# First MLP products of an encoder trunk by seven half-size products in place of eight

## The chip, the cores and the metric

The kernel runs on one core of a Trainium2 chip. A core has TensorE (PE, matrix products; PEld in the profile is its loading of stationary operands), VectorE (DVE), ScalarE (ACT), GpSimd (POOL) and SyncE (SP), and 16 DMA engines which take transfers issued by SP, ACT and POOL. The metric is the time of one execution on the device in microseconds (us), the median of several runs.

## The reference

A two-layer trunk on 512 tokens of width 1024, all in float32. Layer 0 mixes by a conformer convolution, layer 1 by latent attention under a chunk mask. After its mixer each layer has the same kind of MLP, with 4096 hidden columns; the change concerns its first product.

```python
def squared_relu_mlp(h, w1, w2):
    return jnp.square(jax.nn.relu(h @ w1)) @ w2

for layer in range(DEPTH):
    ...
    m = conformer_conv(hn, ...) if layer < N_A_LAYERS else mla_attention(hn, ...)
    h = h + rms_norm(m, mix_post_g[layer])
    f = squared_relu_mlp(rms_norm(h, ffn_pre_g[layer]), w_ff1[layer], w_ff2[layer])
    h = h + rms_norm(f, ffn_post_g[layer])
```

## The kernel before

**Operands in two parts.** TensorE multiplies numbers in a reduced float format (`F32R`). Each operand is therefore kept as a high part and a low part (`split`, line 791: ScalarE writes the high part, VectorE source minus high), and a product is three matmuls: high x high, low x high, high x low. A weight block of 128 x 1024 floats (512 KB) is loaded from `wts` into a tile `raw`, and split into `wh` and `wl` (`weight`, line 733). For the blocks named by `lo_by_dma` (line 88), ScalarE writes both the high part and its negative, and a DMA on POOL's queue adds the block from memory onto the negative, which gives the low part without VectorE.

**Order.** `Program` records every instruction and plans the order before it is issued. TensorE keeps the order in which the program was recorded; each other engine is ordered by due times that are worked back from TensorE's (`due`, line 408, and `schedule`, line 451), with written-out costs for each operation. An operation recorded with two engines (`nc.binary`) goes to the one that would end it first by these costs. All instructions are issued in one helper, line 640, and so the profile shows that line for all of them; groups are told apart by the names of their tiles.

**Buffers.** Tiles belong to tags with a fixed number of places. `raw` (5 places), `wh` (5) and `wl` (6) are taken in turn: a block may be loaded or split only when the block as many places earlier is done with. `USE` lists the weights in the order in which the products take them. `big` (48 tiles of 128 x 512) holds activations, their parts, the convolution's Toeplitz blocks (loaded from `cw`) and the accumulators; `row` (2 of 128 x 1024) holds gains and a bias repeated along the tokens. `mm` is six banks of PSUM.

**The MLP** (`feed_forward`, line 963). The hidden columns go in four groups q of 1024. For each q come first the first products: eight blocks m of 128 columns, for each 8 steps over the 1024 input columns x 3 matmuls, with 512 tokens in each (operand names `mm<-big,wh` and `mm<-big,wl`, moving operand first). In q = 0 the blocks m = 0 to 3 are done in two halves of 256 tokens, because the later half of the normed input X is not there yet; these four blocks get their low parts by DMA. ScalarE applies relu and square into `Z`, eight tiles by token half, column half and u.

Then come that group's second products (names `mm<-wh,big`): Z times the second weight matrix, two by two quarters in seven products of Strassen's kind (`STRASSEN`, `PRODUCTS`). Their left sides are differences of Z tiles made and split by VectorE and ScalarE (`terms`), their right sides are sums of two weight blocks: a plus by a second, accumulating DMA on POOL's queue, a minus by a second `raw` tile and VectorE. In q = 0 ScalarE copies a product into an accumulator in `big`, later VectorE adds onto it (`collect`). A group has 24 loads of 512 KB for its second products, 8 of them accumulating, and 8 for its first.

`post_norm` (line 1065) takes the results, multiplies them by a row of gains (`row`, line 873) and adds them to the residual `h`. `prenorm` transposes and norms `h` into X half by half of the tokens; its last VectorE operation for a half is `SCALAR_TENSOR_TENSOR big<-bc,vt,big`.

Of the kernel before, what the change touches and what calls it, by code (L numbers as in the profile page):

```python
# [8 lines left out]
F32 = mybir.dt.float32  # L9
F32R = mybir.dt.float32r  # L10
# [12 lines left out]
DH = 512  # L23
RMS_EPS = 1e-6
# [98 lines left out]

def _ff(layer):
    for q in range(4):
        for m in range(8):
            _blk(("ff1", layer, q, m))
# [516 lines left out]
def trunk(ctx: ExitStack, tc: tile.TileContext, xT, xN, wts, vec, along, rope, cw, out):  # L644
# [13 lines left out]
    RAW = tag("raw", 5, [P, D], fifo=True)  # L658
    ROW = tag("row", 2, [P, D])
    for t in (RAW, ROW):  # L660
        for place in range(1, t.count):
            t.make(f"{t.name}_", F32, place)
# [7 lines left out]
    BIG = tag("big", 48, [P, T])  # L670
# [61 lines left out]

    def weight(key):

        while key not in blocks:
            name, parts = USE[len(blocks)]
            i, n = BLK[parts[0][0]], _cols[BLK[parts[0][0]]]
# [109 lines left out]
    def sums(parts, t0, dim):  # L847
# [11 lines left out]
    def rsqrt_bc(accs, t0, n, dim, eps, dst=None):  # L859

        nb = n // P
        sm = sums([(b, acc, b) for acc in accs for b in range(nb)], t0, dim)
# [7 lines left out]

    HALVES = {HA: (0, 1), HB: (2, 3)}
# [35 lines left out]
    def residual(F, g, b, dh, o, st, on, r2):  # L907
# [5 lines left out]
        nc.binary(on, out=F[b][dh], in0=F[b][dh], in1=g[:, dh * DH : (dh + 1) * DH], op=ALU.mult)  # L913
# [48 lines left out]

    def feed_forward(layer, X, F):
# [5 lines left out]
        both = {}  # L969
        for q in range(4):  # L970

            Z = {(th, kh): [big() for _ in range(2)] for kh in range(2) for th in range(2)}
            order = [(m, FULL) for m in range(8)]
            if q == 0:
                order = [(m, t) for t in (HA, HB) for m in range(4)] + order[4:]
            for m, (t0, n) in order:
                pt = products(("ff1", layer, q, m), X, t0, n)
                s = slice(t0, t0 + n)
                z = tmp()
                nc.scalar.activation(z[:, s], pt[:, :n], AF.Relu)  # L980
                for th, (a, w) in enumerate((HA, HB)):
                    if t0 <= a < t0 + n:
                        j = m % 2
                        nc.scalar.activation(
# [713 lines left out]
```

## Time and profile before

| | us |
|---|---|
| median of 3 runs | 1059.95 |
| lowest and highest | 1058.62, 1062.92 |
| profiled execution | 1060.22 |
| its span, first to last instruction | 1058.4 |
| layer 0: first products of q = 0 start | 195.26 |
| second products of q = 0 start | 241.97 |
| first products of q = 1 start | 280.05 |
| second products of q = 1 start | 323.57 |
| first products of q = 2 start | 361.65 |

The mean granted TensorE clock is 0.997 of full speed. The starts are read from the timeline of TensorE, where the names of the operands change places. A matmul's line shows start, length and count: matmuls overlap, so that the distance between starts, not the length, is what one costs. A window's line shows, for a stretch, the time in which each engine was busy. A group's line shows how many instructions of one kind there were, their busy time together and the mean length of one in ns, and then the idle time ahead of them with what ended it.

### The profile page before, as it was taken

How to read it: one execution, taken by the hardware profiler on the slowest of the kernel's cores; microseconds unless marked ns; L12 is line 12 of the kernel's file. 1: busy time of each engine (PE TensorE's matmuls, PEld its weight loads, DVE VectorE, ACT ScalarE, POOL GpSimd, SP SyncE). 2: the span in 40 equal slices, each digit the busy share in tenths (PEclk: the TensorE clock that was granted, in tenths of full speed). 3: DMA queues.
4: the chain of work that ended last, by engine and by line, in shares of the span. 5: the costliest groups of instructions: out<-in, count | busy, mean ns of one | idle time of the engine just before them, and what ended most of it. 6: DMA issues, size and time to landing. Idle time of an engine off the chain costs nothing.

```text
span 1058.4 us, 15181 instructions
## 1 busy us (share of the span) xinstructions
PE 1037.9 (98%) x5284; PEld 883.2 (83%) x5284; DVE 763.0 (72%) x1559; ACT 641.6 (61%) x1343; POOL 141.5 (13%) x165
## 2 busy tenths in 40 slices
PE   8999999999999999999999999999999999999996
PEld 7888988988888888888788888889888888888885
DVE  6498994857448738959988977447574495498698
ACT  8552596867556445555767877558575554455652
POOL 1110001101100100002105533301010010000010
PEclk9999999999999999999999999999999999999998
DMA  8996898658857948658822132567598488586694
GB/s 281 319 250 192 271 254 217 163 142 235 250 150 213 259 131 253 180 176 235 225 64 89 56 102 81 177 181 177 162 250 248 119 237 256 148 242 172 180 244 133
DMA packets 67613, 204.08 MB, mean 193 GB/s; under 512 B 7632, under 2 KB 13904, under 8 KB 67536
## 3 DMA queue, kind: packets, MB, share of 16 engines
q1 hardware_dynamic: 49680, 150.15, 41.3%
q0 software_dynamic: 13536, 49.29, 25.7%
q10 hardware_dynamic: 4320, 3.68, 1.1%
q8 instruction: 41, 0.67, 0.3%
q14 instruction: 36, 0.29, 0.1%
HBM read 197.58 MB, written 5.51 MB: 192 GB/s over the span
## 4 chain that ended last, share of the span: by engine, by line
PE 85%; DVE 7%; DMA 3%; ACT 3%; issue 1%; DVEq 0%; ACTq 0%
PE mm L640 82%; DVE big L640 5%; PE bc L640 3%; DMA raw<-wts 2%; ACT big L640 2%; DVE stat L640 1%; DVE wl L640 1%; ACT wh L640 1%; ACT wl L640 1%; DMA uu<-dealt 1%; DMA dealt<-big 1%; DVE tmp L640 0%; ACT tmp L640 0%; DVE h L640 0%; DMA vt<-vec 0%
## 5 line engine op out<-in xcount | busy, mean ns | idle before, releaser
L640 PE MATMUL mm<-big,wh 128*128 128x512 f32 (+1 forms) x1512 | 440.6, 374 | 1.1 <-ACT wh L640 1.1
L640 PE MATMUL mm<-wh,big 128*128 128x512 f32 (+1 forms) x1216 | 372.2, 385 | 0.0
L640 ACT ACTIVATE wh<-raw 128x512 fp32r<-128x512 f32 (+2 forms) x444 | 251.4, 614 | 121.6 <-PE mm L640 73.5
L640 PEld LDWEIGHTS mm<-big,wh 128*128 128x128 f32 x1512 | 276.8, 189 | 50.8 <-ACT wh L640 1.4
L640 DVE TENSOR_TENSOR wl<-raw,wh 128x512 fp32r<-128x512 f32 (+1 forms) x356 | 227.2, 679 | 105.9 <-ACT wh L640 105.5
L640 PE MATMUL mm<-big,wl 128*128 128x512 f32 (+1 forms) x756 | 282.4, 374 | 0.0
L640 PEld LDWEIGHTS mm<-wh,big 128*128 128x128 f32 x1216 | 226.1, 188 | 44.2 <-ACT wh L640 0.2
L640 PE MATMUL mm<-wl,big 128*128 128x512 f32 (+1 forms) x608 | 233.4, 385 | 0.0
L640 PEld LDWEIGHTS mm<-big,wl 128*128 128x128 f32 x756 | 143.1, 189 | 24.6 <-DVE wl L640 0.5
L640 PEld LDWEIGHTS mm<-wl,big 128*128 128x128 f32 x608 | 114.2, 188 | 22.5 <-DVE wl L640 0.4
L640 POOL DMA_DIRECT2D raw<-wts x64 | 55.5, 867 | 568.1 <-DVE wl L640 194.3
L640 ACT ACTIVATE big<-tmp 128x256 f32<-128x256 f32 (+1 forms) x208 | 95.8, 493 | 47.5 <-DVE tmp L640 41.5
L640 DVE TENSOR_TENSOR big<-big,big 128x512 f32<-128x512 f32 (+4 forms) x103 | 69.7, 697 | 55.2 <-ACT big L640 54.9
L640 ACT ACTIVATE tmp<-mm 128x512 f32<-128x512 f32 (+1 forms) x75 | 41.7, 555 | 101.4 <-PE mm L640 100.2
L640 PE MATMUL mm<-big,big 128*128 128x256 f32 (+3 forms) x520 | 83.5, 310 | 1.9 <-DVE big L640 1.9
L640 PEld LDWEIGHTS mm<-big,big 128*128 128x128 f32 x520 | 73.1, 190 | 7.0 <-DVE big L640 2.4
L640 ACT ACTIVATE big<-mm 128x512 f32<-128x512 f32 (+5 forms) x106 | 56.6, 537 | 32.0 <-PE mm L640 30.8
L640 DVE TENSOR_TENSOR big<-tmp,big 128x512 fp32r<-128x512 f32 (+1 forms) x96 | 60.7, 640 | 15.3 <-ACT big L640 12.7
L640 DVE SCALAR_TENSOR_TENSOR big<-big,vt,big 128x512 fp32r<-128x512 f32 (+29 forms) x95 | 63.2, 728 | 5.7 <-ACT big L640 5.7
L640 DVE TENSOR_TENSOR big<-big,mm 128x512 f32<-128x512 f32 x96 | 63.2, 679 | 2.4 <-PE mm L640 2.3
L640 DVE TENSOR_TENSOR tmp<-big,big 128x512 f32<-128x512 f32 x80 | 53.2, 684 | 8.8 <-ACT big L640 8.7
L640 POOL DMA_DIRECT2D wl<-wts x30 | 26.1, 869 | 210.0 <-ACT wl L640 168.7
(90 smaller groups left out, 769.3 us busy)
## 6 DMA issues: line engine op xcount, KB each, us to landing
raw<-wts SPq DMA_DIRECT2D x222, 512.0 KB, 4.9
raw<-wts POOLq DMA_DIRECT2D x64, 512.0 KB, 8.1
wl<-wts POOLq DMA_DIRECT2D x30, 512.0 KB, 8.5
big<-cw SPq DMA_DIRECT2D x45, 256.0 KB, 5.5
big<-wts SPq DMA_DIRECT2D x12, 256.0 KB, 4.3
row<-along SPq DMA_DIRECT2D x5, 512.0 KB, 5.5
raw<-wts SPq DMA_DIRECT2D x12, 192.0 KB, 2.8
big<-xT SPq DMA_DIRECT2D x8, 256.0 KB, 4.6
```

Source lines behind the costliest of these rows:

```text
L640: return f(*args, **kwargs)
```

## The change

In each layer the first products of q = 0 and q = 1 are now computed ahead of all second products of that layer. The eight blocks of a group are regrouped into two units u of 512 hidden columns, with weight blocks of 512 input columns by 256 hidden columns (`w1`, four to a unit, the same bytes as before). The first unit of a layer (q = 0, u = 0) is computed plainly in halves of 256 tokens. The other three units are computed by Winograd's form of Strassen's product: seven products of 512 input columns x 256 hidden columns x 256 tokens. Three of these (1, 2, 4) take a single weight block, and they come first; four (5, 7, 6, 3) take sums that VectorE forms in place in the `raw` tiles. Products 1 and 2 get their low parts by DMA. The combinations of X are formed once per layer, after the plain unit has been recorded: 16 sums of high and low part on POOL or VectorE, 8 operations on VectorE and 16 splits of 256 columns. VectorE and ScalarE combine the seven products, with relu and square, into the same Z tiles.

To hold this, `raw` grows from 5 to 8 places, `big` shrinks from 48 to 46, and the tag `row` goes: a row is now two tiles of `big`, loaded when the first result is taken up. q = 2 and q = 3 stay as they were. The rest of the diff renames a helper, moves a definition and lays out the weights.

```diff
+H = 256
...
-    if name[0] == "ff1":
-        return name[2] == 0 and name[3] < 4
+    if name[0] == "w1":
+        return name[2:4] == (0, 0) or name[4] in LO_BY_DMA
...
+QUADS = ((0, 0), (0, 1), (1, 0), (1, 1))
+EARLY = (0, 1)
+PLAIN = {1: (0, 0), 2: (0, 1), 4: (1, 1)}
+WINOGRAD = (1, 2, 4, 5, 7, 6, 3)
+LO_BY_DMA = (1, 2)
+def _first(layer, q):
+    n = len(USE)
+    for u in range(2):
+        for mh, kh in QUADS:
+            _blk(("w1", layer, q, u, mh, kh))
+    del USE[n:]
+    for u in range(2):
+        for key in QUADS if (q, u) == (0, 0) else WINOGRAD:
+            USE.append((("w1", layer, q, u, key), None))
 def _ff(layer):
+    for q in EARLY:
+        _first(layer, q)
     for q in range(4):
-        for m in range(8):
+        for m in range(8 if q not in EARLY else 0):
...
-    RAW = tag("raw", 5, [P, D], fifo=True)
-    ROW = tag("row", 2, [P, D])
+    RAW = tag("raw", 8, [P, D], fifo=True)
...
-    BIG = tag("big", 48, [P, T])
+    BIG = tag("big", 46, [P, T])
...
+    sums = {}
+    def first_weight(name):
+        _, layer, q, u, key = name
+        def at(mh, kh):
+            return wts[BLK["w1", layer, q, u, mh, kh]]
+        def load(part):
+            t = nc.tile(RAW)
+            nc.sync.dma_start(out=t, in_=at(*part))
+            return t
+        if isinstance(key, tuple):
+            raw, src = load(key), at(*key)
+        elif key in PLAIN:
+            raw, src = load(PLAIN[key]), at(*PLAIN[key])
+            sums[key] = raw
+        else:
+            if key == 5:
+                sums[5], sums[7] = sums[4], load((1, 0))
+            if key == 6:
+                sums[6] = sums[5]
+            if key == 3:
+                sums[3] = sums[6]
+            raw = sums[key]
+            nc.vector.tensor_tensor(out=raw, in0=raw, in1=sums[{5: 7, 7: 1, 6: 1, 3: 2}[key]], op=ALU.add)
+        hi, lo = nc.tile(WH, F32R), nc.tile(WL, F32R)
+        if lo_by_dma(name):
+            for dst, scale in ((lo, -1.0), (hi, 1.0)):
+                nc.scalar.activation(dst, raw, AF.Copy, scale=scale)
+            nc.gpsimd.dma_start(out=lo, in_=src, accum_op=ALU.add)
+        else:
+            split(raw, slice(0, D), (hi, lo))
+        return hi, lo
...
     def row(name):
-        t = nc.tile(ROW)
+        ts = [big() for _ in range(2)]
         nc.early = 30000.0
-        nc.sync.dma_start(out=t, in_=along[ROWS.index(name)])
+        for dh, t in enumerate(ts):
+            nc.sync.dma_start(out=t, in_=along[ROWS.index(name), :, dh * DH : (dh + 1) * DH])
         nc.early = 0.0
-        return t
+        return ts
...
+    def combinations(X):
+        raw = {}
+        for kh, th in QUADS:
+            for kp in range(2):
+                a = raw[kh, th, kp] = big()
+                for j in range(2):
+                    hi, lo = (x[:, th * H : (th + 1) * H].bitcast(F32) for x in X[4 * kh + 2 * kp + j])
+                    nc.binary(("gpsimd", "vector"), out=a[:, j * H : (j + 1) * H], in0=hi, in1=lo, op=ALU.add)
+        out = {p: [] for p in WINOGRAD}
+        for k, (hi, lo) in enumerate(X):
+            out[1 if k < 4 else 2].append((hi[:, :H], lo[:, :H]))
+            if k > 3:
+                out[3].append((hi[:, H:], lo[:, H:]))
+        def put(p, c):
+            for j in range(2):
+                x = big(F32R)
+                out[p].append((x[:, :H], x[:, H:]))
+                split(c, slice(j * H, (j + 1) * H), out[p][-1], slice(0, H))
+        c7 = [tmp() for _ in range(2)]
+        for kp in range(2):
+            b11, b12, b21, b22 = (raw[kh, th, kp] for kh, th in QUADS)
+            nc.vector.tensor_tensor(out=c7[kp], in0=b22, in1=b12, op=ALU.subtract)
+            nc.vector.tensor_tensor(out=b12, in0=b11, in1=b12, op=ALU.subtract)
+            nc.vector.scalar_tensor_tensor(out=b22, in0=b12, scalar=-1.0, in1=b22, op0=ALU.mult, op1=ALU.subtract)
+            nc.vector.scalar_tensor_tensor(out=b21, in0=b22, scalar=-1.0, in1=b21, op0=ALU.mult, op1=ALU.subtract)
+        for p in WINOGRAD[2:-1]:
+            for kp in range(2):
+                put(p, {4: raw[1, 0, kp], 5: raw[0, 1, kp], 7: c7[kp], 6: raw[1, 1, kp]}[p])
+        return out
+    def rectified(z, src, sign=1.0):
+        nc.scalar.activation(z, src, AF.Relu, scale=sign)
+        nc.scalar.activation(z, z, AF.Square)
+    def first_plain(layer, X, Z):
+        for t0, n in (HA, HB):
+            for mh in range(2):
+                Z[t0 // n, mh][0] = big()
+                for mm in range(2):
+                    pt = nc.tile(MM)
+                    for kh in range(2):
+                        hi, lo = weight(("w1", layer, 0, 0, (mh, kh)))
+                        for kk in range(4):
+                            ws, x = slice(kk * H + mm * P, kk * H + (mm + 1) * P), X[4 * kh + kk]
+                            for j, (a, b) in enumerate(((hi, x[0]), (lo, x[0]), (hi, x[1]))):
+                                nc.tensor.matmul(
+                                    pt[:, :n], lhsT=a[:, ws], rhs=b[:, t0 : t0 + n],
+                                    start=(kh == kk == j == 0), stop=(kh == 1 and kk == 3 and j == 2),
+                                )
+                    rectified(Z[t0 // n, mh][0][:, mm * H : (mm + 1) * H], pt[:, :n])
+    def first_winograd(layer, q, u, XC, Z):
+        def product(p):
+            pt = nc.tile(MM)
+            hi, lo = weight(("w1", layer, q, u, p))
+            for kk, x in enumerate(XC[p]):
+                for mm in range(2):
+                    ws = slice(kk * H + mm * P, kk * H + (mm + 1) * P)
+                    for j, (a, b) in enumerate(((hi, x[0]), (lo, x[0]), (hi, x[1]))):
+                        nc.tensor.matmul(
+                            pt[:, mm * H : (mm + 1) * H], lhsT=a[:, ws], rhs=b,
+                            start=(kk == mm == j == 0), stop=(kk == 3 and mm == 1 and j == 2),
+                        )
+            return pt
+        def add(out, a, pt):
+            nc.vector.tensor_tensor(out=out, in0=a, in1=pt, op=ALU.add)
+        for quad in QUADS:
+            Z[quad][u] = big()
+        c11, c21, c12, c22 = (Z[quad][u] for quad in QUADS)
+        u2, u3 = tmp(), tmp()
+        nc.scalar.activation(u2, product(1), AF.Copy)
+        add(c11, u2, product(2))
+        rectified(c11, c11)
+        nc.scalar.activation(c21, product(4), AF.Copy)
+        p5, p7 = product(5), product(7)
+        add(u2, u2, product(6))
+        add(u3, u2, p7)
+        add(c22, u3, p5)
+        add(c12, u2, p5)
+        rectified(c22, c22, -1.0)
+        add(c21, c21, u3)
+        rectified(c21, c21, -1.0)
+        add(c12, c12, product(3))
+        rectified(c12, c12)
...
+        early = {q: {quad: [None, None] for quad in QUADS} for q in EARLY}
+        first_plain(layer, X, early[0])
+        XC = combinations(X)
+        for q, u in ((0, 1), (1, 0), (1, 1)):
+            first_winograd(layer, q, u, XC, early[q])
         for q in range(4):
-            Z = {(th, kh): [big() for _ in range(2)] for kh in range(2) for th in range(2)}
-            order = [(m, FULL) for m in range(8)]
-            if q == 0:
-                order = [(m, t) for t in (HA, HB) for m in range(4)] + order[4:]
-            for m, (t0, n) in order:
-                pt = products(("ff1", layer, q, m), X, t0, n)
-                s = slice(t0, t0 + n)
+            if q in early:
+                Z = early[q]
+            else:
+                Z = {quad: [big() for _ in range(2)] for quad in QUADS}
...
+            for m in range(8 if q not in early else 0):
...
+            if isinstance(g, str):
+                g = row(g)
...
-            hold = h + [nc.tile(ROW)]
-            for b, t in enumerate(hold):
+            brow = [big() for _ in range(2)]
+            for b, t in enumerate(h + brow):
                 nc.vector.tensor_copy(out=t[:, 0:1], in_=u[:, 0:1])
-                nc.sync.dma_start(out=t, in_=xN[b] if b < TB else along[ROWS.index("b_pw2")])
-            brow = hold[TB]
```

More of the change, by code (lines that the diff above doesn't have):

```diff
@@ L861, in rsqrt_bc @@
         nb = n // P
[L862 removed]
+        sm = row_sums([(b, acc, b) for acc in accs for b in range(nb)], t0, dim)
         st = nc.tile(STAT)
@@ L1352, in latent @@
             raw.append(a)
-        sm = sums([(b, acc, b) for b in range(nb)], t0, dim)
+        sm = row_sums([(b, acc, b) for b in range(nb)], t0, dim)
         st = nc.tile(STAT)
```

51 lines of the change are left out of this document (30 added, 21 removed).

## Prediction

> **What bounds the kernel now.** I read the page's shares of the engines first, then the chain that ended last, then the waits of TensorE.
>
> ```profile
> span 1058.4 us, 15181 instructions
> ...
> PE 1037.9 (98%) x5284; PEld 883.2 (83%) x5284; DVE 763.0 (72%) x1559; ACT 641.6 (61%) x1343; POOL 141.5 (13%) x165
> ...
> PE 85%; DVE 7%; DMA 3%; ACT 3%; issue 1%; DVEq 0%; ACTq 0%
> ...
> PE mm L640 <- DVE big L640: 1.9, 3, 0.8
> ```
>
> TensorE (PE) works in 98% of the span, and its longest wait in total is 1.9 us. So the time is the sum of its matmuls, as long as the other engines keep feeding it. That has to be read by stage. In the windows below the columns are: stretch, its length, busy us and count of PE, PEld, DVE, ACT and POOL, granted clock, DMA share, GB/s. The four stretches are layer 0's q 0 and q 1: first products, second products, first, second.
>
> ```profile
> 195.30:241.90 46.60, 46.60 (x305) 42.78 (x304) 31.88 (x77) 34.21 (x83) 3.45 (x4) 1.00 0.66 176
> 241.90:280.00 38.10, 38.10 (x170) 31.55 (x169) 24.80 (x40) 26.81 (x51) 3.45 (x4) 1.00 0.89 253
> 280.00:323.00 43.00, 43.00 (x191) 35.59 (x191) 18.96 (x30) 21.25 (x45) 3.45 (x4) 1.00 0.62 162
> 323.00:361.50 38.50, 38.50 (x172) 31.87 (x171) 34.09 (x56) 21.57 (x40) 3.45 (x4) 1.00 0.88 257
> ```
>
> PE never idles here. But first products are light on VectorE (DVE) and DMA (18.96 of 43 us, share 0.62), and second products heavy (34.09 of 38.5 us, 0.88). The old order alternates them, so a light stage fills the buffers for the heavy one. The new order puts q 0's and q 1's second products back to back.
>
> **The matmuls removed.** Full-width and half-width products stand side by side in the trace of before:
>
> ```profile
> 292.07 0.62 PE L640 MATMUL mm<-big,wh 128*128 128x512 f32 x2
> 292.52 0.39 PE L640 MATMUL mm<-big,wl 128*128 128x512 f32 x1
> 292.75 0.62 PE L640 MATMUL mm<-big,wh 128*128 128x512 f32 x2
> ...
> 211.43 0.40 PE L640 MATMUL mm<-big,wh 128*128 128x256 f32 x2
> 211.67 0.28 PE L640 MATMUL mm<-big,wl 128*128 128x256 f32 x1
> 211.79 0.40 PE L640 MATMUL mm<-big,wh 128*128 128x256 f32 x2
> ```
>
> Three of 512 columns start every 0.68 us, 226.7 ns each; three of 256 every 0.36 us, 120 ns each. A unit (one q, one u: 512 hidden columns, all tokens) was 4 blocks x 8 x 3 = 96 full-width matmuls, 21.76 us; it becomes 7 products x 4 x 2 x 3 = 168 half-width ones, 20.16 us. That saves 1.60 us a unit. There are three units a layer (the fourth stays plain, 192 half-width matmuls as before), six in all: **-9.6 us**. Nothing else of PE's is added or removed.
>
> The Trainium skill ("TensorE: Matmul & The Clock Gate", Back-to-back issue gap) gives a sustained 81 ns at N = 128 and 131 ns at N = 512, and N/2.4 + 2.5 ns for an isolated matmul. Between the first two, N = 256 would cost some 98 ns, a unit 16.4 us against 12.6, and the change would lose 23 us (an estimate from that page); by the formula it would save 14.2 us. The rows agree with neither, and they decide.
>
> **What is added on VectorE.**
>
> ```profile
> 224.38 2.49 DVE L640 TENSOR_TENSOR wl<-raw,wh 128x512 fp32r<-128x512 f32 x4
> ...
> L640 DVE TENSOR_TENSOR wl<-raw,wh 128x512 fp32r<-128x512 f32 x347 | 223.4, 685 | 105.1 <-ACT wh L640 104.7
> ...
> L640 DVE TENSOR_TENSOR big<-tmp,big 128x256 fp32r<-128x256 f32 x16 | 6.4, 419 | 2.0 <-ACT tmp L640 2.0
> ```
>
> Four of 512 columns in a row take 2.49 us, so 0.60 us each; 256 columns fewer take 0.266 us off the mean, so one of 1024 columns is some 1.13 us, and one of 256 some 0.40 us (6.4/16). A unit adds 4 sums of weight blocks and 5 low parts (two of seven come by DMA), 9 x 1.13 = 10.2, and 7 sums of products, 4.2: 14.4 us of DVE in 20.16 us of PE. The old unit took 8 x 0.60 = 4.8 us, or nothing where the low parts came by DMA. Each layer adds the combinations of X: 8 x 0.60 + 16 low parts x 0.40 = 11.2 us, and 16 sums hi + lo on POOL or DVE, 6.4 us if on DVE.
>
> ScalarE is not late: per unit 9 conversions of about 1.0 us (0.624 us at 512 and 0.408 at 256 give 0.84 ns a column) and 10 operations of about 0.58 us, 14.8 of 20.16 us.
>
> ```profile
> L640 ACT ACTIVATE wh<-raw 128x512 fp32r<-128x512 f32 x416 | 239.3, 624 | 120.9 <-PE mm L640 73.5 <-DMA raw<-wts 17.2 <-issue 12.1
> ...
> L640 ACT ACTIVATE wh<-raw 128x256 fp32r<-128x256 f32 x16 | 6.5, 408 | 0.7 <-DMA raw<-wts 0.7
> ```
>
> **Does DVE fit beside PE?** The place to look is the first half-size unit.
>
> ```profile
> 208.18 0.88 DVE L640 SCALAR_TENSOR_TENSOR big<-bc,vt,big 128x256 fp32r<-128x256 f32 x2
> 208.97 0.35 DVE L640 SCALAR_TENSOR_TENSOR stat<-stat 128x2 f32<-128x2 f32 x2
> ...
> 220.42 0.40 PE L640 MATMUL mm<-big,wl 128*128 128x512 f32 x1
> ```
>
> X is complete at 209.06 us. The plain products end at 220.4, and the unit's last product (3) would start 6 x 2.88 = 17.3 us later, at 237.7: DVE has 28.6 us. It must do 2.3 us of small norm operations (13 like the second row, 0.175 us each), 11.2 us of combinations, 10.2 us of weights and one sum, 0.6: 24.3 us. With all sums hi + lo on DVE it is 30.7 us and PE waits 2.1 us; with the half of the early tokens done sooner, 27.5 us and no wait. I take 1.5 us a layer, near the first end, since DVE was busy in the stage before too: **+3.0 us**. The bounds are 0 and, by rival B, 12 us a layer.
>
> From there to the end of q 1's second products PE needs 11.4 + 60.5 + 76.2 = 148 us. DVE's count: 2.3 + 17.6 + 43.2, and for second products 56 instructions in q 0 (10 differences and 14 low parts of the left sides, 4 differences and 28 low parts of weights) and 70 in q 1 (14 sums into the accumulators more) at 0.60, 75.6: 139 us, 94%. Within the pair of second stages, 75.6 less some 8 us done ahead (four weight pairs, two products' terms) is 67 of 76.2 us, 88%, the density of 34.09 in 38.5 that PE survived before. So I cost the rest at nothing; it is tight, and its cover is only the four pairs.
>
> **DMA.** The same weight blocks are read, plus two low parts a unit through POOL's queue: 12 transfers of 512 KB, and POOL issues them among the accumulating loads of the second products. q 1's first blocks now pass q 0's second blocks on SP's queue.
>
> ```profile
> q1 hardware_dynamic: 49680, 150.15, 41.3%
> q0 software_dynamic: 13536, 49.29, 25.7%
> ...
> raw<-wts SPq DMA_DIRECT2D x222, 512.0 KB, 4.9
> ...
> wl<-wts POOLq DMA_DIRECT2D x30, 512.0 KB, 8.5
> ```
>
> One 512 KB read costs 437 us / 286 = 1.53 us of all engines on the hardware queue and 272/94 = 2.9 us on POOL's. A low part lands 8.5 us after its issue. It can be begun when the pair six places earlier is free, 5 x 2.88 = 14.4 us ahead, so it is in time. The pair of second stages is what matters: 2 x 24 reads in 76.2 us, plus two for the next stage. The window of q 1's old second stage moved 257 GB/s, 0.49 blocks a us, at share 0.88. So 76.2 us bring 37 blocks, and 13 must be there at the start. I count 14: eight for the four pairs converted ahead (products 3 and 6), and six of the next, as the raw buffers of the last unit come free only in its last 12 us (12 x 0.49). I take nothing, with 2.2 us to spare; rival A is the other end.
>
> **Buffers.** Rows of gains and of the bias move from ROW into BIG, which shrinks from 48 to 46 and holds two for the bias through the convolution.
>
> ```profile
> 50.89 61.53 SPq L640 DMA_DIRECT2D big<-cw  x35
> 115.20 0.38 SPq L640 DMA_DIRECT2D big<-cw  x1
> ...
> 132.07 0.61 PE L640 MATMUL mm<-uu,big 128*128 128x128 f32 x4
> ```
>
> There the Toeplitz blocks load as BIG comes free, 1.76 us apart; four tiles fewer delay them by some 7 us. The last one had 16.9 us, less 5.5 to land: 11 us. I take 0, bounds 0 and 7.
>
> **Sum.** The profiled execution took 1060.2 us (span 1058.4 and 1.8 around it), 0.3 above the median of 1059.95: 1060.2 - 9.6 + 3.0 = **1053.6 us**.
>
> **The rivals.**
>
> A, slower: the pair of second stages outruns DMA. If only 9 blocks are ahead at its start, 41 take 41/0.49 = 83.7 us, 7.5 us more than PE: 1053.6 + 15 = 1068.6. It decides below 13 blocks, and from 11 down the kernel is slower than before. For it: share 0.89 already, and accumulating loads land late. Against: three more raw buffers, and the lighter units before. Chance 0.24, one third of it short of +0.5%.
>
> B, the sums hi + lo go to POOL and hold DVE up.
>
> ```profile
> 206.13 0.15 DVE L640 TENSOR_TENSOR stat<-stat 128x2 f32<-128x2 f32 x1
> ...
> 583.26 1.45 DVE L640 TENSOR_TENSOR stat<-stat 128x4 f32<-128x4 f32 x2
> 584.75 1.56 DVE L640 SCALAR_TENSOR_TENSOR stat<-stat 128x4 f32<-128x4 f32 x2
> ...
> 583.21 1.28 POOL L640 TENSOR_TENSOR big<-big,big 64x512 fp32r<-64x512 f32 x1 [1.09 <-ACT big L640]
> 584.57 2.95 POOL L640 TENSOR_TENSOR wl<-raw,wh 128x256 fp32r<-128x256 f32 x3
> ```
>
> Two tiny operations, 0.15 us each when alone, last 1.45 us together beside a POOL addition. At about 1 us each (2.95/3), 16 additions hold 16 us of DVE in place of 6.4, up to 12 us a layer late; at 5 us the time is 1053.6 + 2 x 3.5 = 1060.6. Against: the planner chooses whichever ends first. Chance 0.16, a third of it slower by over 0.5%. The Trainium skill ("SBUF — State Buffer", two separate sides) calls the pair of ports that POOL shares with DVE an exclusive lock for the whole instruction; these rows agree.
>
> C, the convolution waits for its blocks: half of the 7 us, 1057.6. Chance 0.15.
>
> D, half-width matmuls come out limited by loading weights (190 ns instead of 120): 168 x 0.07 a unit, +71 us. 192 matmuls a layer already ran at 120 ns; chance 0.01. Another 0.02 is for planning anew elsewhere.
>
> **How the numbers follow.** A measurement here tells 0.5% (5.3 us) from no change: 1054.65 and 1065.25. The forecast (up to 1 us more lost, down to the floor of 1050.6) has 0.42, all faster. A gives 0.08 the same and 0.16 slower, B 0.11 and 0.05, C 0.15 the same, the rest 0.02 and 0.01: faster 0.42, same 0.36, slower 0.22. The range runs from 1050 (just under the floor) to 1067, which leaves out most of A beyond it; the likeliest's own is 1050.6 to 1054.6.
>
> **What would show it.** Right: half-width matmuls 120 ns apart, 504 more a layer; PE busy near 1028; DVE above 90% in 209 to 357 us; waits of PE of 1 to 2 us at product 6 or 3 of each layer's first unit. A shows as PE waiting for converted weights, these for raw blocks, in q 1's second stage; B as long small DVE operations under POOL additions at 200 to 220 us; C as PE waiting at 100 to 135 us for cw. The forecast is wrong if PE's waits in either layer's pair exceed 3 us.

## Result and profile after

The changed kernel took 1078.36 us (median of 4 runs, 1077.53 to 1078.69), the kernel before on the same chip 1059.35 us. The ratio is 1.017 (95% interval 1.0148 to 1.0191): slower by 18 us, where 1053.6 was forecast and the range ended at 1067. The page of the changed kernel, first lines and its chain:

```profile
span 1076.6 us, 16282 instructions
...
PE 1035.6 (96%) x5716; PEld 899.1 (84%) x5716; DVE 851.7 (79%) x1675; ACT 679.6 (63%) x1353; POOL 158.5 (15%) x190
...
PE 67%; DVE 9%; ACT 3%; issue 1%; DVEq 0%; ACTq 0%
```

TensorE has 432 matmuls more, as it should (6 units of 168 in place of 96). It is busy 2.3 us less than before, and idle for 1076.6 - 1035.6 = 41.0 us in place of 20.5. Where the idle time lies is read from the starts of the stages in TensorE's timeline. "Last second products" are those of q = 3, and a stage ends where the next begins.

| stage, us | before | after | difference |
|---|---|---|---|
| start to layer 0's first products (convolution) | 195.26 | 216.57 | +21.31 |
| to layer 0's last second products (MLP) | 280.63 | 277.06 | -3.57 |
| to layer 1's first products (attention) | 242.88 | 244.70 | +1.82 |
| to layer 1's last second products (MLP) | 280.88 | 279.42 | -1.46 |
| the rest of the span | 58.75 | 58.85 | +0.10 |

So the MLPs, which the change is about, came out 5.0 us shorter (6.6 were forecast: 9.6 less 3.0), and the loss lies in the convolution, whose operations the change doesn't touch. Its windows, before and then after (columns as in the prediction: stretch, length, busy us and count of PE, PEld, DVE, ACT, POOL, clock, DMA share, GB/s):

```profile
40.00:60.00 20.00, 20.00 (x90) 16.57 (x89) 16.93 (x26) 7.56 (x13) 1.72 (x2) 1.00 1.05 333
60.00:100.00 40.00, 38.37 (x206) 32.80 (x205) 37.17 (x57) 20.82 (x42) 3.45 (x4) 1.00 0.79 219
...
120.00:140.00 20.00, 20.00 (x182) 20.00 (x181) 19.50 (x42) 16.74 (x39) 2.59 (x3) 1.00 0.82 207
140.00:160.00 20.00, 18.77 (x110) 15.96 (x109) 19.06 (x76) 18.91 (x40) 1.72 (x2) 1.00 0.85 267
```

```profile
40.00:60.00 20.00, 20.00 (x90) 16.57 (x89) 7.94 (x12) 6.87 (x12) 1.43 (x2) 1.00 1.01 350
60.00:100.00 40.00, 34.03 (x173) 28.58 (x172) 40.00 (x62) 18.94 (x40) 3.75 (x5) 0.93 0.67 154
...
120.00:140.00 20.00, 20.00 (x175) 19.71 (x174) 18.16 (x36) 13.60 (x31) 2.59 (x3) 1.00 1.03 330
140.00:160.00 20.00, 9.04 (x64) 8.88 (x63) 7.71 (x22) 10.26 (x26) 0.86 (x1) 0.74 1.05 334
```

Two things differ. **First,** VectorE works 7.94 of the 20 us from 40 to 60, in place of 16.93. It then is busy for all of 60 to 100 and can't catch up, and TensorE is idle there for 6.0 us (1.6 before). **Second,** DMA is full (shares 1.03 and 1.05) from 120 to 160, where before it had 0.82 and 0.85, and TensorE stands for 11 of the last 20 us. What stopped VectorE is seen in the timelines of ScalarE and then of VectorE (start, length, what, and in brackets the idle time ahead and what ended it):

```profile
44.55 0.82 ACT L661 ACTIVATE big<-big,vt 128x512 f32<-128x512 f32 x1 [0.31 <-DVE big L661]
55.44 0.33 ACTq L661 DMA_DIRECT2D dealt<-big  x1
55.81 1.16 ACT L661 ACTIVATE wl<-raw 128x512 fp32r<-128x512 f32 x2 [10.44 <-DMA big<-cw]
```

```profile
45.01 2.72 DVE L661 SCALAR_TENSOR_TENSOR big<-big,vt,big 128x510 f32<-128x510 f32 x4
57.61 5.34 DVE L661 SCALAR_TENSOR_TENSOR big<-big,vt,big 128x509 f32<-128x509 f32 x8 [9.89 <-ACT big L661]
```

What SP had issued in that time:

```profile
46.81 8.21 SPq L661 DMA_DIRECT2D big<-cw  x9
```

ScalarE also issues transfers. From 45.4 to 55.4 us it stood ahead of the issue of `dealt<-big`, the transfer that deals a convolution tile out over the partitions, and what let it go was the landing of a `big<-cw` load, which has nothing to do with that tile. The reason stands in the built program, and the trace's semaphores show it: the transfers of SP and ScalarE take eight semaphores in turn, and each issue waits until the transfer eight before it has landed. In the changed kernel that was a Toeplitz block, the second of the nine above, issued at 47.49 us and landed at 55.36; the work queued behind it on ScalarE then starved VectorE for 9.89 us. The Trainium skill ("DMA: Bandwidth & Descriptors", Anatomy of one DMA — SWDGE (gpsimd) path) says that a DMA's semaphore wait is done by the issuing sequencer and not by the DMA engines. That section follows a transfer issued by GpSimd; these rows show the same for one issued by ScalarE, at 10 us. In the kernel before the same transfer went out at 47.85.

The second loss shows in TensorE's timeline:

```profile
113.38 8.20 PE L661 MATMUL mm<-uu,big 128*128 128x128 f32 x72
...
152.00 10.26 PE L661 MATMUL mm<-uu,big 128*128 128x128 f32 x72 [10.96 <-DMA uu<-dealt]
```

The last convolution block waited 10.96 us for its dealt operand (`uu`, 64 KB a transfer). The last of these transfers was issued at 138.5 and took 13.4 us to land. Its issue, too, had stood behind a semaphore: that of a 512 KB load issued at 129.72, which landed at 138.50.

### The profile page after: what moved, and what is told of

Read it like the earlier page. It is cut to its first block, busy times and chain, and to the rows that moved or that the text cites. A ratio compares the mean times of both kernels' runs of the same rounds, so it can differ in the third digit from the quotient of the medians.

```text
span 1076.6 us, 16282 instructions
## 1 busy us (share of the span) xinstructions
PE 1035.6 (96%) x5716; PEld 899.1 (84%) x5716; DVE 851.7 (79%) x1675; ACT 679.6 (63%) x1353; POOL 158.5 (15%) x190
## 4 chain that ended last, share of the span: by engine, by line
PE 67%; DVE 9%; ACT 3%; issue 1%; DVEq 0%; ACTq 0%
PE mm L661 66%; DVE big L661 6%; ACT big L661 2%; PE bc L661 1%; DVE stat L661 1%; DVE wl L661 1%; ACT junk L661 1%; DVE h L661 1%; ACT wh L661 0%; ACT wl L661 0%; DVE tmp L661 0%; DVEq L1857 0%; ACT tmp L661 0%; ACTq L661 0%; DVE wq L661 0%
## 5 line engine op out<-in xcount | busy, mean ns | idle before, releaser
L661 PE MATMUL mm<-big,wh 128*128 128x256 f32 (+1 forms) x1800 | 444.6, 337 | 1.4 <-ACT wh L661 1.3
L661 ACT ACTIVATE wh<-raw 128x512 fp32r<-128x512 f32 (+3 forms) x430 | 269.6, 665 | 151.7 <-PE mm L661 105.0
L661 PEld LDWEIGHTS mm<-big,wh 128*128 128x128 f32 x1800 | 309.8, 191 | 36.7 <-ACT wh L661 1.6
L661 DVE TENSOR_TENSOR wl<-raw,wh 128x512 fp32r<-128x512 f32 (+3 forms) x340 | 236.3, 724 | 91.1 <-ACT wh L661 90.6
L661 PE MATMUL mm<-big,wl 128*128 128x256 f32 (+1 forms) x900 | 302.3, 336 | 0.7 <-DVE wl L661 0.7
L661 PEld LDWEIGHTS mm<-big,wl 128*128 128x128 f32 x900 | 171.6, 191 | 18.8 <-DVE wl L661 1.9
L661 DVE TENSOR_TENSOR big<-big,big 128x512 f32<-128x512 f32 (+5 forms) x179 | 110.6, 640 | 18.1 <-ACT junk L661 12.7
L661 ACT ACTIVATE big<-tmp 128x512 fp32r<-128x512 f32 (+2 forms) x152 | 76.0, 522 | 23.7 <-DVE tmp L661 20.0
L661 ACT ACTIVATE big<-big 128x512 f32<-128x512 f32 (+4 forms) x152 | 82.9, 573 | 10.9 <-DVE big L661 6.0
L661 PE MATMUL mm<-uu,big 128*128 128x128 f32 x360 | 44.6, 289 | 14.1 <-DMA uu<-dealt 11.0
```

What stands on the lines that cost most here:

```text
L661: return f(*args, **kwargs)
```

## The experiments

Their base and label are named in each. The start of layer 0's first products is called the end of the convolution (195.26 before, 216.57 after). Runs of the kernel before beside them had medians of 1060.2 to 1061.2 us.

**1. Which half of the change loses? buffers_alone** is the kernel before with the changed kernel's buffers (raw 8, big 46, rows and bias in `big`) and the old MLP:

```diff
-    RAW = tag("raw", 5, [P, D], fifo=True)
-    ROW = tag("row", 2, [P, D])
+    RAW = tag("raw", 8, [P, D], fifo=True)
...
-    BIG = tag("big", 48, [P, T])
+    BIG = tag("big", 46, [P, T])
```

> The old MLP with the new buffers alone: raw 8, big 46, rows and bias in big. Theory 1 (the loss lies in the convolution and comes from the buffers): the first products of layer 0 start about 21 us later than before, at 215 to 218 us, and the time is before plus 19 to 23 us, 1079 to 1082. Theory 2 (the loss comes with the new MLP, whose work reaches back into the convolution through the shared engines): the convolution ends as before, 195 us, and the time stays within 3 us of before, 1057 to 1062.

Measured: 1084.72 us, ratio 1.0227 (1.0202 to 1.0252), some 3 us over theory 1's range; the convolution ended at 215.22. The loss is there without the new MLP. **mlp_alone** is the reverse, the new MLP with raw 5, row 2 and big 48:

> The new MLP with the old buffers: raw 5, row 2, big 48. Theory 1: the convolution ends as before (195 us, give or take 2), and the MLPs bring the 4 to 5 us that they bring beside the new buffers (3.6 in layer 0, 1.5 in layer 1), less what raw 5 costs the half-size units: 1053 to 1058. Theory 2: the convolution is late here too, and the time is 1074 to 1080.

Measured: 1077.74 us, ratio 1.0165 (1.0139 to 1.0191). The convolution ended at 198.46, but the MLPs grew by 7.6 and 4.7 us over before (288.27 and 285.56). TensorE's waits say why:

```profile
PE mm L661 <- ACT wh L661: 8.2, 11, 1.4
PE mm L661 <- DVE wl L661: 4.1, 6, 1.1
```

ScalarE itself waited 14.8 us for raw blocks in layer 0's MLP (4.5 in the changed kernel). So five places of `raw` don't carry the half-size units; the longer `raw` is needed by the change, and the expectation took its price far too small.

**2. The issue on ScalarE. deal_on_pool** is the changed kernel with every engine's order left as it was; only the dealing transfers (`dealt<-big` and `uu<-dealt`) are issued by POOL instead of ScalarE:

```diff
+            engine = getattr(op, "emit", engine)
...
-        nc.scalar.dma_start(out=dr.rearrange("p r m -> p (r m)"), in_=up)
+        ops = [nc.scalar.dma_start(out=dr.rearrange("p r m -> p (r m)"), in_=up)]
...
+        for op in ops:
+            op.emit = "gpsimd"
```

> The changed kernel in the same order, but the convolution's transfers (dealt and uu) are issued by POOL instead of ScalarE. Theory 1a (the first 10 us of the convolution's loss are ScalarE standing behind the issue of a transfer which waits for a load of cw, so that VectorE starves from 47.7 to 57.6 us): VectorE's gap of 9.9 us goes, and the time is 7 to 12 us under the changed kernel's, 1066 to 1071. Theory 1b (the loads themselves are late, whoever issues): VectorE still idles there, and the time stays within 3 us of 1078.

Measured: 1064.7 us, ratio 1.0045 (1.0031 to 1.0058); the convolution ended at 204.00, 12.6 us earlier. VectorE's gap is gone; TensorE still waits for the last `uu` (timeline of VectorE, and waits of TensorE):

```profile
45.74 7.99 DVE L662 SCALAR_TENSOR_TENSOR big<-big,vt,big 128x510 f32<-128x510 f32 x12
```

```profile
PE mm L662 <- DMA uu<-dealt: 7.5, 1, 7.5
```

The control, **before_deal_on_pool**, makes the same edit in the kernel before:

> The kernel before, in its own order, with the convolution's transfers issued by POOL. If POOL's issue only takes away what the new plan brought (ScalarE held behind one issue from 45 to 55 us), this kernel, where ScalarE was held from 53 to 62 us with VectorE busy all the same, stays within 3 us of before, 1057 to 1063. If issuing from POOL is quicker in itself, it is 4 to 10 us faster, 1050 to 1056, and the gain of deal_on_pool says nothing on the change.

Measured: 1057.5 us, ratio 0.9964 (0.9946 to 0.9982), the convolution 3.1 us earlier (192.15). So of the 12.6 us, 9.5 are the change's own.

**3. Tiles. raw7_big48** is the changed kernel with raw 7 and big 48; **lazy_bias** takes the bias row (two tiles of `big`) only when it is used:

```diff
-    RAW = tag("raw", 8, [P, D], fifo=True)
+    RAW = tag("raw", 7, [P, D], fifo=True)
...
-    BIG = tag("big", 46, [P, T])
+    BIG = tag("big", 48, [P, T])
```

```diff
-            brow = [big() for _ in range(2)]
-            for b, t in enumerate(h + brow):
+            for b, t in enumerate(h):
...
+            brow = brow or row("b_pw2")
```

raw7_big48:

> The changed kernel with raw 7 and big 48, rows and bias still in big. If the convolution is short of big tiles, it ends within 3 us of before (195 us) and the time is 1054 to 1059. If the deeper raw prefetch is what crowds the loads, 7 places are nearly as bad as 8: first products of layer 0 at 210 to 217 us and 1070 to 1078.

lazy_bias:

> The changed kernel, but the bias row takes its two tiles of big only when the second pointwise product is reached, so that the convolution has 46 tiles of big in place of 44. Theory 2a (big is short in the convolution, the last cw loads come 12 us late and meet the raw loads, so that the last block's uu transfers land 11 us late): TensorE's wait for uu of 11 us falls to under 4 and the time to 1066 to 1072, while VectorE's gap of 10 us stays. Theory 2b (the raw prefetch of 8 places crowds the transfers): the wait stays above 8 us and the time within 4 us of 1078.

Measured: raw7_big48 1063.82 us, ratio 1.0038 (1.0024 to 1.0051), convolution ended at 199.06; but the MLPs took 280.09 and 279.96, so most of their gain went. Both theories missed: the time lies between their ranges. lazy_bias 1078.52 us, ratio 1.0166 (1.0139 to 1.0193), convolution 217.80: two tiles more during the convolution gave it nothing, so a shortage of tiles alone is not the cause.

**4. Where a first hint of the plan came from.** Two kernels put the sums of high and low part (`combinations`) on VectorE alone, with the dealing on POOL; **deal_lazy_vector** has lazy_bias too.

```diff
-                    nc.binary(("gpsimd", "vector"), out=a[:, j * H : (j + 1) * H], in0=hi, in1=lo, op=ALU.add)
+                    nc.binary(("vector",), out=a[:, j * H : (j + 1) * H], in0=hi, in1=lo, op=ALU.add)
```

deal_pool_sums_vector:

> deal_on_pool with the sums hi + lo of the combinations on VectorE only. If POOL's additions hold VectorE up by the shared port (four h operations took 6.1 us beside them in layer 1, 2.7 us without), layer 1's stretch from its first products to its last second products goes from 279.4 to 276 to 278 us, layer 0's stays at 277 give or take 1, and the time is 1 to 4 us under deal_on_pool's, 1061 to 1064. If VectorE's own load is the bound there, 6.4 us more work a layer makes it slower: 1065 to 1070.

deal_lazy_vector:

> All three mends in the changed kernel: transfers of the convolution issued by POOL, the bias row taken late, sums on VectorE. If the three causes stand apart, the convolution ends within 3 us of before (195 us), the MLPs keep 3 to 4 us each, and the time is 1052 to 1057, under both kernels. If the convolution's loss has another cause in the deeper raw prefetch, it is 1058 to 1064.

Measured: deal_pool_sums_vector **1053.52 us, ratio 0.9932 (0.9906 to 0.9959)**, faster than both kernels and the fastest of all that ran, and 7.5 us under the range that was expected of its sums; deal_lazy_vector 1058.1 us, ratio 0.998 (0.9966 to 0.9994), as expected if the longer `raw` has a loss of its own. The convolution, which these sums don't touch, ended at 193.63 in the first and at 199.47 in the second, and at 204.00 in deal_on_pool. `run` (line 607 before, 628 after) makes 16 plans, each from the due times of the one before it, and keeps the one that it thinks shortest. As built, the changed kernel, buffers_alone, mlp_alone, lazy_bias and deal_lazy_vector run the **first** plan; the kernel before runs the fourteenth, raw7_big48 the seventh, deal_pool_sums_vector the twelfth.

**5. The plan by itself.** Four kernels of one chip. changed_later_plan and deal_on_pool_later_plan may not take the first plan; changed_last_plan takes the sixteenth; before_first_plan is the kernel before with the first.

```diff
-            if best is None or span < best[0]:
+            if _ and (best is None or span < best[0]):
```

changed_last_plan has, in the same place:

```diff
-            if best is None or span < best[0]:
+            if _ == 15:
```

before_first_plan makes one plan alone:

```diff
-    def run(self, tags, rounds=16):
+    def run(self, tags, rounds=1):
```

changed_later_plan:

> The changed kernel, buffers and all operations as they are; only the planner may not take the first of its 16 plans (the changed kernel runs that one; the kernel before runs the fourteenth). Theory P (the loss in the convolution comes from which plan was taken, and not from the number of tiles): first products of layer 0 start at 195 to 201 us in place of 216.57, the wait of TensorE for uu<-dealt falls from 11 to under 4 us, the time is 1057 to 1063. Theory T (46 tiles are too few for the convolution): they start at 210 or later, the time is 1072 or more.

changed_last_plan:

> As changed_later_plan, but with the sixteenth plan, a second sample of the later ones. Theory P: first products of layer 0 start at 195 to 203 us, and the time is within 5 us of changed_later_plan. Theory T: 210 us or later, 1072 or more.

before_first_plan:

> The kernel before, but with the first of its 16 plans in place of the fourteenth. Theory P: its convolution loses too, first products of layer 0 start at 203 to 217 us in place of 195.26, and the time is 1066 to 1080. Theory T: with its 48 tiles and the rows apart it starts at 195 to 200, 1058 to 1064.

deal_on_pool_later_plan:

> deal_on_pool (the dealing transfers issued by POOL), but not with the first plan; sums of high and low part on POOL or VectorE as in the changed kernel. It separates the two things that deal_pool_sums_vector changed, its plan and its sums. If the plan made its gain: 1052 to 1056, first products of layer 0 at 192 to 196 us. If the sums on VectorE did: 1060 to 1065, at 202 us or later.

| kernel | us | ratio (95%) | convolution ended |
|---|---|---|---|
| changed_later_plan | 1069.96 | 1.0095 (1.0069 to 1.0121) | 199.78 |
| changed_last_plan | 1068.17 | 1.0085 (1.0058 to 1.0112) | 197.98 |
| before_first_plan | 1079.96 | 1.0183 (1.0148 to 1.0218) | 201.07 |
| deal_on_pool_later_plan | 1061.7 | 1.0008 (0.9993 to 1.0024) | 193.44 |

With a later plan the convolution ends 17 to 19 us earlier, with the same tiles and operations: theory P holds for it. Against P's numbers, TensorE's wait for `uu` in changed_later_plan came to 4.3 us and not under 4, and the time didn't fall as far as 1057 to 1063, because other stages gave some back (attention 249.87 us in changed_later_plan, 244.70 in the changed kernel). deal_on_pool_later_plan is split: its convolution came out as if the plan had made the gain, its time as if the sums had. And the first plan cost the kernel before only 5.8 us in the convolution, not the 8 to 22 expected; its other 14 us lie in all later stages (2.7, 5.0, 2.0 and 4.2). What the two plans do differently shows in SP's timeline, where its transfers are issued; the changed kernel first, then changed_later_plan:

```profile
101.00 16.80 SPq L661 DMA_DIRECT2D big<-cw  x12
117.85 0.42 SPq L661 DMA_DIRECT2D raw<-wts  x1
118.78 1.64 SPq L661 DMA_DIRECT2D big<-cw  x2
121.33 0.33 SPq L661 DMA_DIRECT2D raw<-wts  x1
124.52 0.33 SPq L661 DMA_DIRECT2D big<-cw  x1
125.85 0.33 SPq L661 DMA_DIRECT2D raw<-wts  x1
126.27 0.38 SPq L661 DMA_DIRECT2D big<-cw  x1
127.17 0.33 SPq L661 DMA_DIRECT2D raw<-wts  x1
127.59 1.53 SPq L661 DMA_DIRECT2D big<-cw  x1
```

```profile
106.43 13.92 SPq L661 DMA_DIRECT2D big<-cw  x16
120.40 1.87 SPq L661 DMA_DIRECT2D raw<-wts  x4
```

The first plan puts loads of 512 KB among the last Toeplitz blocks, so that these end at 129 us in place of 120, and both run into the dealing of the last block.

**6. What the tiles cost, and how far plans lie apart.** With later plans for both MLPs and both buffers:

buffers_alone_later_plan:

> buffers_alone (the MLP as before, raw 8, big 46, rows in big), but not with the first of its plans. If the plan is what cost it 22 us: the convolution ends 2 to 5 us later than before (197 to 201 us at the start of the first products), the time is 1061 to 1068. If 46 tiles are too few whatever the plan: 210 us or later, 1075 or more.

before_last_plan:

> The kernel before with its sixteenth plan in place of the fourteenth. It gives the distance between two later plans of one kernel: I expect under 5 us (1056 to 1065), its first products of layer 0 within 4 us of 195.26. If plans as such scatter by 10 us or more, it comes out over 1070 and the differences of a few us between other kernels say little.

Measured: buffers_alone_later_plan 1068.59 us, ratio 1.0082 (1.0057 to 1.0107), convolution 198.13; before_last_plan 1064.31 us, ratio 1.004 (1.0021 to 1.0058), convolution 198.48. Four later plans with 46 tiles (199.78, 197.98, 198.13 and sums_vector_later_plan's 200.37) end the convolution where two later plans with 48 do (198.48, 199.06), and 195.26 is the kernel before. Two later plans of one unchanged kernel lie 3.2 us apart in the convolution and 4 us in the whole.

**7. Which size acts with the first plan?** buffers_alone with the first plan, raw 7 and big 48 in one (the edit of part 3), and in the other:

```diff
-    RAW = tag("raw", 8, [P, D], fifo=True)
+    RAW = tag("raw", 5, [P, D], fifo=True)
```

first_plan_raw7_big48:

> buffers_alone (MLP as before, rows in big), first plan, but raw 7 and big 48. If the longer raw is what acts with the first plan (its loads stand among the last Toeplitz blocks, and the issue of dealt stands behind one of these): first products of layer 0 start at 208 us or later, TensorE waits over 5 us for uu<-dealt. If the 46 tiles do: 198 to 203 us.

first_plan_raw5_big46:

> buffers_alone, first plan, but raw 5 (as in the kernel before) and big 46. If the longer raw acts: 198 to 204 us, and the wait for uu<-dealt under 5 us. If the 46 tiles do: 210 us or later.

Measured: raw 7 with big 48: 1076.4 us, ratio 1.0145 (1.0122 to 1.0167), convolution 210.22. Raw 5 with big 46: 1076.18 us, ratio 1.0143 (1.0103 to 1.0182), convolution 202.69. Both waits for `uu` were 5.4 us, one of them against the expectation. In ScalarE's timeline the issue of `dealt` moves with `raw` and not with the tiles, raw 7 first:

```profile
54.94 0.33 ACTq L640 DMA_DIRECT2D dealt<-big  x1
55.31 1.16 ACT L640 ACTIVATE wl<-raw 128x512 fp32r<-128x512 f32 x2 [9.71 <-DMA big<-cw]
```

```profile
48.27 0.33 ACTq L640 DMA_DIRECT2D dealt<-big  x1
48.70 1.16 ACT L640 ACTIVATE wl<-raw 128x512 fp32r<-128x512 f32 x2 [4.95 <-DMA big<-cw]
```

So it is the longer `raw` that acts with the first plan. More places let its loads go out earlier, among the Toeplitz blocks, and shift the turn of the semaphores so that `dealt` stands behind a later one. The late issue of `dealt` comes with the longer `raw` in a later plan too (53.77 us in changed_later_plan); there it costs less, as part 8 shows.

**8. The sums, by themselves. sums_vector_later_plan** is changed_later_plan with the sums on VectorE alone:

> changed_later_plan with the sums of high and low part on VectorE alone. If POOL's additions hold VectorE up (rival B): layer 0's and layer 1's first products (start to start of the second products) take 85.4 us each in place of 88.2 and 87.9, and the time falls by about 5 us, to 1061 to 1066. If it was the plan: no difference over 1 us in these stretches.

Measured: 1060.3 us, ratio 1.0001 (0.9985 to 1.0017). Windows over the first products of layer 0 and layer 1, changed_later_plan and then this:

```profile
199.80:288.00 88.20, 86.96 (x722) 86.20 (x721) 81.17 (x136) 70.85 (x130) 18.16 (x23) 1.00 0.66 173
728.50:816.40 87.90, 85.72 (x713) 85.28 (x712) 80.62 (x130) 68.01 (x122) 19.69 (x26) 1.00 0.67 177
```

```profile
200.40:285.70 85.30, 85.30 (x713) 85.23 (x712) 76.74 (x142) 67.01 (x122) 8.70 (x10) 1.00 0.69 180
722.30:807.60 85.30, 85.30 (x714) 85.23 (x713) 75.46 (x138) 66.57 (x123) 9.53 (x11) 1.00 0.70 182
```

With the sums on VectorE the stretches are 2.9 and 2.6 us shorter, TensorE never idles in either, and VectorE is busy *less*. With POOL, TensorE stood idle for 1.2 and 2.2 us of them (88.20 - 86.96 and 87.90 - 85.72); in layer 0 a part of the rest is work, eight more of the norm's transposes that this plan puts into the stretch. The planner takes the third plan for the one kernel and the twelfth for the other, so a share of the plan in these differences isn't excluded. Of the 8.3 us between the two spans, 4.3 lie in the attention (245.53 in place of 249.87), which was planned otherwise and shows nothing of the sums.

This run has a twin. deal_pool_sums_vector takes the twelfth plan too, and TensorE, VectorE and ScalarE run the same operations in the same order in both traces; only the issue of the dealing differs. It alone takes the convolution from 200.37 to 193.63 us and the ratio from 1.0001 to 0.9932. So with the plan held fixed, issuing from ScalarE costs 6.7 us here, in the kernel before 3.1.

**9. Two tiles back in the fastest version. deal_sums_raw7** (raw 7, big 48):

> The fastest version (dealing transfers issued by POOL, sums on VectorE) with raw 7 and big 48 in place of 8 and 46, not with the first plan. If the two tiles still cost the convolution: 1050 to 1053. If the eighth raw place feeds the pair of second stages: 1054 to 1058, with the loss in 280 to 350 us.

Measured: 1055.53 us, ratio 0.9953 (0.9934 to 0.9973). Both came in part: the convolution ended 2.3 us earlier (191.31), and each MLP took 1.8 us more (278.25 and 278.31 against 276.47 and 276.43). From 270 to 472 us ScalarE waited 10.6 us for raw blocks, in deal_pool_sums_vector not at all. The two kernels run different orders, and 2.3 us is less than two plans of one kernel lie apart in the convolution. It doesn't beat deal_pool_sums_vector.

## Why the prediction was wrong, step by step

**The step that failed is "Buffers", "I take 0, bounds 0 and 7".** The term was the convolution, and it measured +21.3 us. The place of rival C was right and its mechanism wrong: TensorE waited for `uu` at 141 to 152 us, not for `cw` at 100 to 135. The prediction asked whether four tiles fewer let the last Toeplitz block come in time, as if the order of the loads stayed. It didn't: a change of any size makes the planner order the whole kernel anew. And the size that acted is not the one that it priced: the longer `raw`, which it counted only as a help against rival A, put loads among the Toeplitz blocks and `dealt` behind them. Its 0.02 "for planning anew elsewhere" was where the result lay. With the runs of parts 2 and 5 the 21.3 us come apart:

| what | from | us |
|---|---|---|
| ScalarE held by the issue of `dealt`, beyond that of before | (216.57 - 204.00) - (195.26 - 192.15) | 9.5 |
| the first plan, with that taken away | 204.00 - 193.44 | 10.6 |
| what is left: the sizes, the new MLP, another plan | 193.44 - 192.15 | 1.3 |

The order of the subtraction matters, since plan and hold act on each other: with ScalarE issuing, a later plan alone gives back 17 to 19, and the hold then costs only 3.2 more than in the kernel before (199.78 - 193.44, less 3.1). The last line holds what the step had tried to price at 0 to 7. It is no more than plans differ among themselves, so nothing is shown of the tiles' cost but that it is small.

**Matmuls removed, -9.6: right.** TensorE's timeline in the first products:

```profile
244.19 0.28 PE L661 MATMUL mm<-big,wl 128*128 128x256 f32 x1
244.31 0.40 PE L661 MATMUL mm<-big,wh 128*128 128x256 f32 x2
244.55 0.28 PE L661 MATMUL mm<-big,wl 128*128 128x256 f32 x1
```

Three in 0.36 us, 120 ns each. The first products of q 0 and q 1 took 46.71 + 43.52 = 90.23 us in layer 0 before, and 85.35 in sums_vector_later_plan where TensorE never idles: -4.9 us for a predicted -4.8. Rival D is out. "PE busy near 1028" came out at 1035.6. TensorE was granted less clock after its waits (last section), 0.989 over the run in place of 0.997; deal_pool_sums_vector, at 0.997, was busy for 1030.4, so about 2 us stay open. "504 more a layer" is a slip: 504 is all that the three units have, 288 of the old kind go, and 216 more a layer is what the page shows (432 in all).

**VectorE late in the first unit, +1.5 us a layer: the size came out by luck, the place and the cause were rival B's.** In the changed kernel the first products took 86.54 and 87.71 us, 1.2 and 2.4 over those of sums_vector_later_plan. But no product 6 or 3 waited; the norm of X did. And where VectorE had all the sums, for which the prediction counted a wait of 2.1 us, TensorE didn't wait at all. In layer 1, VectorE beside POOL after, and then VectorE in the same place before, where POOL had nothing:

```profile
743.84 6.13 DVE L661 SCALAR_TENSOR_TENSOR h<-big,stat,h 128x512 f32<-128x512 f32 x4
```

```profile
744.33 3.10 POOL L661 TENSOR_TENSOR big<-big,big 128x256 f32<-128x256 f32 x4
```

```profile
723.18 2.74 DVE L640 SCALAR_TENSOR_TENSOR h<-big,stat,h 128x512 f32<-128x512 f32 x4
```

The same four operations take 6.13 us beside four POOL additions, and 2.74 alone: 3.4 us for 3.1 us of POOL. That agrees with the rule that the prediction took from the Trainium skill ("SBUF — State Buffer", two separate sides). B's 3.5 us a layer was of the right order in changed_later_plan (2.9 and 2.6 longer, 1.2 and 2.2 of it idle).

**The pair of second stages, cost nothing: right in the time, and rival A's waits did not come.** Windows over each layer's two second stages back to back:

```profile
303.10:371.10 68.00, 68.00 (x302) 56.31 (x301) 63.74 (x105) 50.11 (x93) 10.36 (x12) 1.00 0.97 281
...
826.00:894.20 68.20, 68.20 (x303) 56.31 (x302) 63.38 (x104) 49.10 (x92) 10.36 (x12) 1.00 0.98 284
```

TensorE works throughout, DMA at 0.97 and VectorE at 63.74/68 = 94% (88% was forecast): as tight as feared, and it held. The window is 68 us and not 76 because q 2's first products begin among the last of q 1's second ones, until 388 us in layer 0: in the plan a matmul that isn't ready lets later ones pass. That TensorE keeps the recorded order, as the section on the kernel says, holds only for those that are ready. So 36 of the pair's 336 products came late by the plan, and first products of q 2 filled their place, a cover that the prediction didn't count. Fewer places of raw cost more here: 1.8 us a layer at 7, though by another plan, and with 5 the MLPs were longer than before (parts 9 and 1).

**Attention, not in the sum: +1.8 us,** and between 241.0 and 249.9 us in the runs, by the plan. Nothing finer was tried.

**The rivals' prices.** C's "half of the 7 us" is 1057.1 and not 1057.6; nothing hangs on it.

**The range** took its upper end from rival A and had no term for the plan. The whole gap of the unchanged kernel between two plans, 1060 to 1080 us, was wider than it. The forecast 1053.6 was met by deal_pool_sums_vector (1053.52), but by luck: its twin with the dealing on ScalarE took 1060.3, no less than the kernel before. With the dealing on POOL in both, the change gains 4.0 us (1057.5 to 1053.52), no more than two plans of one kernel lie apart in the whole. The MLPs alone are 4.2 and 5.1 us shorter there than in before_deal_on_pool (280.64 and 281.52), more than the 0.3 and 1.1 by which they differ between the two later plans of the kernel before; the attention gives 4.6 us back.

## What to carry to other kernels

Where an order is planned by a program, a change of buffer sizes changes the order everywhere, also in stages that it doesn't touch: compare the built orders of the untouched stages, force another plan as a control, and hold no gain that is smaller than two plans of one kernel lie apart. An engine that computes is a bad place for issuing a transfer whose semaphore is shared in turn with loads: ten microseconds of its queue hung here on a transfer that had nothing to do with it. An addition given to POOL was not free here when VectorE read two tiles beside it.

## What the runs showed of the hardware

Here a wait of TensorE cost more than its length. Windows of the changed kernel after the 11 us wait:

```profile
152.00:156.00 4.00, 4.00 (x19) 4.00 (x20) 0.00 (x0) 0.00 (x0) 0.00 (x0) 0.50 1.04 420
156.00:160.00 4.00, 4.00 (x37) 4.00 (x37) 0.69 (x1) 3.60 (x10) 0.00 (x0) 0.98 1.02 408
```

For the first 4 us after it the granted clock is 0.50 and 19 matmuls start, in the next 4 us 37. The 72 matmuls took 10.26 us in place of 8.20, so the wait cost 13 us. The Trainium skill ("TensorE: Matmul & The Clock Gate", Part 1: The HAM clock gate) gives half the clock after an idle window and about 3.4 us of sustained work until it is full; these rows agree, at about 4 us.

The small transfers took longer with a fuller DMA: the last 64 KB of `uu` took 13.4 us at a share of 1.05, and the median of the twenty was 5.3 us against 2.3 before (rows of the DMA view, after and before):

```profile
uu<-dealt ACTq DMA_DIRECT2D x20, 64.0 KB, 5.3
```

```profile
uu<-dealt ACTq DMA_DIRECT2D x20, 64.0 KB, 2.3
```
